# Late modulation vectors as row products on VectorE in a hybrid attention / DeltaNet layer

## The chip, the cores and the metric

The kernel runs on one core of a Trainium2 chip. The metric is the device time of one execution in microseconds (us). The engines are TensorE (PE; its weight loads are listed as PEld), VectorE (DVE), ScalarE (ACT), GpSimd (POOL) and SyncE (SP), which issues the DMAs. Each works through its own queue in order; semaphores tie the queues together.

## The reference, cut to what matters

One layer of a diffusion backbone over 512 latent tokens with a prefix of 256 context tokens, 1024 channels wide, in float32. Two modulation vectors of six parts each are made from the condition vectors `c` and `c_ctx`:

```python
mod_lat = jax.nn.silu(c) @ w_mod + b_mod          # (1, 6144)
mod_ctx = jax.nn.silu(c_ctx) @ w_mod + b_mod
sh1, sc1, g1, sh2, sc2, g2 = jnp.split(mod_lat, 6, axis=-1)
hx = modulate(rms_norm(x), sh1, sc1)              # h * (1 + scale) + shift
...
x = x + g1 * merge_branches(attn_x, gdn_x, gate_x, w_pa, w_pd, w_out)
x = x + g2 * conv_ffn(modulate(rms_norm(x), sh2, sc2), w_up, ffn_conv_w, ffn_conv_b, w_down)
```

The shift and scale of the first sub-layer (`sh1`, `sc1`, columns 0 to 2047 of `w_mod`) are needed at once, for latent and context. The other four parts, `g1`, `sh2`, `sc2`, `g2` (columns 2048 to 6143), are needed only for the latent tokens and only behind the output projection, late in the layer: they are the late modulation vectors. They are 4096 dot products of length 1024 over 16 MB of weights.

Between the two stand the input projection, grouped-query attention (8 query heads, 2 key heads), and a bidirectional chunked gated DeltaNet (8 heads), whose results are merged, projected and followed by a gated MLP.

## The kernel before, in words

All of it is one program for the Tile framework: the source names tiles, pools and operations, and a planner orders each engine's queue by a simulated timeline, from the priority of the instructions (program order, unless a block such as `first()` or `sooner()` raises it) and from when data and buffers are free. `keep_in_program_order` pins an instruction behind the one that stands before it on its engine. `pinned[0]` does so for all PE instructions of a stage. A pool's memory is taken again by the next pool that is opened at its place; with `reuse_waits="tile"` a new tile waits only for the old tiles that it overlaps.

Every large matmul is done in three passes, hi x hi, hi x lo and lo x hi, of operands that ACT and DVE split (`split`, L122; weights in `load_w`, L191: one conversion `whi` on ACT, one subtraction `wlo` on DVE).

The stages in the order of the program:

1. Loads and early modulation (pool `m1`, L415 to L583). `xs`, three tiles of context and latent tokens, are loaded first and normalised; `wm`, eight loads of 1 MB, are the early columns of `w_mod`. The order on PE is written out in `ORD` (L37) and pinned; the loads' order is `LORD`.
2. Key, value and query projection (L698 to L757, pool `kvp`). `blk` 0 is keys, 1 values, 2 to 5 pairs of query heads; there are 28 steps (`blk`, `t`), one for each block and tile of 128 tokens. A step is 24 matmuls into `pq`, then rotary work on DVE and ACT (`qt`, `qtmp`), and the transposes `pt` of the step three before (`LAG`, L54), whose result ACT and DVE split into `KH`/`KL` and `QH`/`QL`. `decays` (L591) runs among the steps: betas and decays of the DeltaNet.
3. Attention (`attend`, L825): for each head and tile of 128 queries, scores into the one bank pair `pS`, maximum on DVE, exponential on ACT, then transposes of the probabilities and products with the values (`ab`). Matmuls of the DeltaNet's projections (`fillA`) are filled in between.
4. The DeltaNet with the other projections, then output projection and MLP, which read the late vectors from columns 16 to 47 of `mod` (L1371 to L1381, L1469).

The late vectors are made by `late_mods` (L362), a generator that stage 2 advances by `MK` = 2.6 steps for each of its 28 steps. For each of eight blocks `q` of 512 columns, `part` (L365) loads eight tiles `wmd` of 128x512 (contraction index on partitions), multiplies each with its column of silu(c) (`csl`) and adds them up: four by DVE, four by ACT with the additions on POOL. Two sums `macc` are added on POOL; `total` (L380) sums over the partitions by a matmul with ones, and ACT copies the row of 512; `columns` (L385) turns it by four transposes of one row each, and DVE adds the bias into `mod`. All of `part` is pinned in program order on its engines (`held`, L359).

Of the kernel before, what the change touches and what calls it, by code (L numbers as in the profile page):

```python
# [6 lines left out]
F32 = mybir.dt.float32  # L7
F32R = mybir.dt.float32r
AF = mybir.ActivationFunctionType
# [38 lines left out]
NS = 2  # L48
MV, MT, CT = 0, 6, 9
MACT, MK, MU = 1, 2.6, 0  # L50
MPIN, MB = 1, 5
DA = '11142332'
# [22 lines left out]
S_BMOD, S_CW, S_FW, S_FB, S_GNW, S_FNW, S_C, S_END = 0, 48, 120, 252, 296, 297, 305, 321  # L75
R_QW, R_QS, R_KW, R_KS, R_A, R_DT, R_END = 0, 128, 256, 384, 512, 528, 544


def hybrid_layer_body(tc, x, ctxt, xT, consts, cols, rows, w_mod1, w_mod2, w_db, w_aq, w_cm, w_pa, w_pd, w_out,
# [39 lines left out]
    def act(out, a, f=AF.Copy, **kw):  # L119
        A.activation(out, a, f, **kw)  # L120
# [10 lines left out]
    def mm(ps, a, b, start=True, stop=True):  # L131
        T.matmul(ps, a, b, start=start, stop=stop)

    with es:
# [34 lines left out]
        modc = cp.tile([P, 16], F32, name="modc")  # L169
        csl = cp.tile([P, KT], F32, name="csl")  # L170

# [14 lines left out]
        def xbank():  # L186
            return xps.tile([P, 4, P], F32, name="xb", tag="x")
# [170 lines left out]

        def held(i):  # L359
            return tc.keep_in_program_order(i) if MPIN else i  # L360

        def late_mods():  # L362
            accs = {}

            def part(q, k):  # L365
                if k == 0:
                    accs[q] = [mdp.tile([P, 512], F32, name="macc", tag="macc", bufs=4) for _ in range(2)]
                av, ap = accs[q]
                wk = mdp.tile([P, 512], F32, name="wmd", tag="wmd", bufs=MB)
                SP.dma_start(wk, w_mod2[q, k // 2][:, (k % 2) * 512:(k % 2) * 512 + 512])  # L370
                if k % 2:
                    held(V.scalar_tensor_tensor(out=av, in0=wk, scalar=csl[:, k:k + 1], in1=av, op0=ALU.mult, op1=ALU.add))
                else:
                    held(A.activation((av, ap, wk)[min(k // 2, 2)], wk, AF.Copy, scale=csl[:, k:k + 1]))
                    if k > 2:
                        held(G.tensor_tensor(out=ap, in0=ap, in1=wk, op=ALU.add))
                if k == KT - 1:
                    held((V if MV else G).tensor_tensor(out=ap, in0=ap, in1=av, op=ALU.add))

            def total(q):  # L380
                ps = xbank()[0:1, :, :].rearrange("p a b -> p (a b)")
                mm(ps, ones[:, 0:1], accs[q][1])
                act(accs[q][0][0:1, :], ps)

            def columns(q):  # L385
                pst = xbank()[:, 0, 0:4]
                for i in range(4):
                    T.transpose(pst[:, i:i + 1], accs[q][0][0:1, i * P:(i + 1) * P], ident[0:1, 0:1])
                tt(mod[:, 16 + 4 * q:20 + 4 * q], pst, col[:, S_BMOD + 16 + 4 * q:S_BMOD + 20 + 4 * q], ALU.add)

            for i in range(9 * KT + CT - 7):
                for at, fn in ((MT, total), (CT, columns)):
                    q = (i - KT - at) // KT
                    if (i - at) % KT == 0 and 0 <= q < 8:
                        fn(q)
                if i < 8 * KT:
                    part(i // KT, i % KT)
                yield

        modact, mods = [MACT], late_mods()  # L400

# [13 lines left out]
        with m1_es:  # L415
# [175 lines left out]
        def decays(g1):  # L591
            rowt = g1.tile([P, 32], F32, name="rowt")
            SP.dma_start(rowt, rows[R_A:R_END].partition_broadcast(P))
            trt = g1.tile([P, 2, P], F32, name="trt")
# [63 lines left out]


        at_es = ExitStack()  # L660
        ap_ = at_es.enter_context(tc.tile_pool(name="ap", bufs=1))
# [7 lines left out]
        with kv_es:  # L669
            mdp = kv_es.enter_context(tc.tile_pool(name="mdp", bufs=1, reuse_waits="tile"))  # L670
            kvp = kv_es.enter_context(tc.tile_pool(name="kvp", bufs=1, reuse_waits="tile"))
# [25 lines left out]

            pend, dec, mcount = [], decays(kvp), 0  # L698
            pinned[0] = KPIN
            for blk in range(6):  # L700
                w2 = [load_w(w_aq[blk, i]) for i in range(2)]
                for t in range(6 if blk < 2 else 4):
# [48 lines left out]
            for i in range(FQ):  # L751
                next(fillA, None)
            for _ in mods:
                pass
            while pend:
# [5 lines left out]
        with at_es:  # L761
# [24 lines left out]
            def probs(h, t, pm):  # L786
                if t == 0:
                    hold["ao"] = at2.tile([P, NL], F32, name="ao", tag="ao", bufs=2)
# [3 lines left out]
                ao, PH, PL = hold["ao"], hold["PH"], hold["PL"]  # L792
                sl = slice((t % 2) * P, (t % 2) * P + P)
# [31 lines left out]
            def attend():  # L825
# [686 lines left out]
def _layout(i):  # L1512
# [32 lines left out]
    a["rows"] = f(np.concatenate([qw, sw(qw), kw, sw(kw), np.asarray(i["a_log"])[0].reshape(-1),  # L1545
                                  np.asarray(i["dt_bias"])[0].reshape(-1)]))
# [37 lines left out]
```

## Time and profile before

| | |
|---|---|
| median of 3 runs | 1305.97 us (1303.61 to 1308.03) |
| the profiled execution | 1306.96 us |
| its span on the core | 1304.3 us |
| mean granted clock of TensorE | 0.978 |
| PE busy | 1229.6 us (94%) |
| DVE busy | 848.4 us (65%) |
| ACT busy | 626.3 us (48%) |
| POOL busy | 308.3 us (24%) |
| DMA | 170.80 MB, 131 GB/s on the mean |

The profile is of one execution. Its span reaches from the first to the last instruction of the program; the time of the execution is a little longer. "Busy" is the time in which an engine worked on at least one instruction; matmuls overlap, so PE is called busy until the modelled end of each. A row of a group gives the line of the source (often that of a helper, such as L87 for a matmul, L108 for `tt`, L117 for `stt`, L120 for `act`), the engine, the operation, the tiles out<-in, the shapes, the count, then busy us and mean ns of one, then idle time of the engine before it and what ended it. The chain of waits is followed back from the last instruction to whatever released each.

### The profile page before, as it was taken

How to read it: one execution, taken by the hardware profiler on the slowest of the kernel's cores; microseconds unless marked ns; L12 is line 12 of the kernel's file. 1: busy time of each engine (PE TensorE's matmuls, PEld its weight loads, DVE VectorE, ACT ScalarE, POOL GpSimd, SP SyncE). 2: the span in 40 equal slices, each digit the busy share in tenths (PEclk: the TensorE clock that was granted, in tenths of full speed). 3: DMA queues.
4: the chain of work that ended last, by engine and by line, in shares of the span. 5: the costliest groups of instructions: out<-in, count | busy, mean ns of one | idle time of the engine just before them, and what ended most of it. 6: DMA issues, size and time to landing. Idle time of an engine off the chain costs nothing.

```text
span 1304.3 us, 20850 instructions
## 1 busy us (share of the span) xinstructions
PE 1229.6 (94%) x7835; PEld 1031.3 (79%) x7835; DVE 848.4 (65%) x1625; ACT 626.3 (48%) x1403; POOL 308.3 (24%) x364
## 2 busy tenths in 40 slices
PE   7899999999968999899998999999999999999997
PEld 4487878999857877778787878788988888888886
DVE  5886987777759986685665556555576666663323
ACT  5453656666576665474453443233354444443221
POOL 1752420000143249559447300000000000000000
PEclk8999999999998999899999999999999999999998
DMA  8656631121373342543533555265043222233331
GB/s 321 227 169 197 223 118 62 65 86 50 111 252 105 124 140 91 177 131 110 178 120 116 170 165 168 92 219 190 9 129 97 97 97 95 91 94 97 90 100 65
DMA packets 70789, 170.80 MB, mean 131 GB/s; under 512 B 7872, under 2 KB 18720, under 8 KB 69280
## 3 DMA queue, kind: packets, MB, share of 16 engines
q1 hardware_dynamic: 70688, 169.47, 39.4%
q8 instruction: 61, 1.00, 0.3%
q14 instruction: 40, 0.33, 0.1%
HBM read 144.23 MB, written 25.21 MB: 130 GB/s over the span
## 4 chain that ended last, share of the span: by engine, by line
PE 66%; POOL 10%; DVE 9%; DMA 5%; ACT 4%; issue 3%; SPq 0%; POOLq 0%; DVEq 0%; ACTq 0%
PE mc L87 32%; PE mb L87 17%; PE pq L87 4%; POOL R L108 4%; POOL prod L108 4%; PE pb L87 3%; PE pS L87 3%; PE ab L87 2%; PE ab L91 1%; DMA Gb<-gamdr 1%; PE xb L91 1%; DVE wlo L108 1%; PE pk L87 1%; DMA sz<-gdr 1%; POOL NN L108 1%
## 5 line engine op out<-in xcount | busy, mean ns | idle before, releaser
L108 DVE TENSOR_TENSOR wlo<-wraw,whi 128x1024 fp32r<-128x1024 f32 x152 | 187.6, 1235 | 162.6 <-ACT whi L120 161.6
L120 ACT ACTIVATE whi<-wraw 128x1024 fp32r<-128x1024 f32 x152 | 159.1, 1048 | 205.5 <-PE mc L87 106.5
L87 PE MATMUL mb<-hxH,whi 128*128 128x512 f32 x384 | 165.1, 430 | 2.1 <-DVE R L108 1.9
L87 PE MATMUL mb<-hxL,whi 128*128 128x512 f32 x384 | 155.0, 404 | 0.0
L87 PE MATMUL mb<-hxH,wlo 128*128 128x512 f32 x384 | 154.3, 402 | 0.0
L87 PE MATMUL mc<-h2L,whi 128*128 128x512 f32 (+1 forms) x376 | 142.7, 379 | 0.0
L87 PE MATMUL mc<-h2H,whi 128*128 128x512 f32 (+1 forms) x376 | 142.3, 378 | 0.3 <-ACT whi L120 0.3
L87 PE MATMUL mc<-h2H,wlo 128*128 128x512 f32 (+1 forms) x376 | 140.8, 374 | 0.5 <-DVE wlo L108 0.5
L108 POOL TENSOR_TENSOR rc<-rc,mhalf 128x2 f32<-128x2 f32 x4 | 3.3, 818 | 459.4 <-DVE rc L114 459.4
L87 PEld LDWEIGHTS mb<-hxH,wlo 128*128 128x128 f32 x384 | 74.0, 193 | 18.3
L87 PEld LDWEIGHTS mb<-hxH,whi 128*128 128x128 f32 x384 | 74.6, 194 | 13.9 <-ACT t L120 2.1
L87 PEld LDWEIGHTS mb<-hxL,whi 128*128 128x128 f32 x384 | 74.6, 194 | 10.3
L87 PEld LDWEIGHTS mc<-h2H,whi 128*128 128x128 f32 x376 | 70.6, 188 | 14.9 <-ACT whi L120 0.5
L87 PEld LDWEIGHTS mc<-h2H,wlo 128*128 128x128 f32 x376 | 70.6, 188 | 14.7 <-DVE wlo L108 1.0
L87 PEld LDWEIGHTS mc<-h2L,whi 128*128 128x128 f32 x376 | 70.7, 188 | 12.2
L87 PE MATMUL mc<-aH,whi 128*128 128x512 f32 (+1 forms) x198 | 72.9, 368 | 0.6 <-DVE x L117 0.6
L87 PE MATMUL mc<-aL,whi 128*128 128x512 f32 (+1 forms) x198 | 73.0, 369 | 0.0
L87 PE MATMUL mc<-aH,wlo 128*128 128x512 f32 (+1 forms) x198 | 72.0, 364 | 0.0
L117 DVE SCALAR_TENSOR_TENSOR u<-mc,col,u 128x511 f32<-128x511 f32 x88 | 65.3, 746 | 1.4
L108 POOL TENSOR_TENSOR prod<-X,R 128x31 f32<-128x31 f32 (+15 forms) x93 | 53.5, 576 | 22.3 <-DVE X L108 15.4
L108 POOL TENSOR_TENSOR R<-R,prod 128x31 f32<-128x31 f32 (+15 forms) x93 | 57.1, 613 | 6.8
L87 PE MATMUL pq<-whi,hxH 128*128 128x256 f32 x192 | 56.6, 295 | 0.0
(354 smaller groups left out, 3078.3 us busy)
## 6 DMA issues: line engine op xcount, KB each, us to landing
wraw<-in_w_cm_dram SPq DMA_DIRECT2D x48, 512.0 KB, 3.9
wraw<-in_w_up_dram SPq DMA_DIRECT2D x44, 512.0 KB, 3.7
wmd<-in_w_mod_dram SPq DMA_DIRECT2D x64, 256.0 KB, 3.8
wm<-in_w_mod_dram SPq DMA_DIRECT2D x8, 1024.0 KB, 8.2
wraw<-in_w_down_dram SPq DMA_DIRECT2D x16, 512.0 KB, 3.5
wraw<-in_w_aq_dram SPq DMA_DIRECT2D x12, 512.0 KB, 4.8
M<-gamdr SPq DMA_DIRECT2D x64, 64.0 KB, 4.4
wraw<-in_w_pa_dram SPq DMA_DIRECT2D x8, 512.0 KB, 4.0
```

Source lines behind the costliest of these rows:

```text
L87: i = nc.tensor.matmul(*a, **k)
L91: i = nc.tensor.transpose(*a, **k)
L108: (eng or V).tensor_tensor(out=out, in0=a, in1=b, op=op)
L117: V.scalar_tensor_tensor(out=out, in0=a, scalar=s, in1=b, op0=op0, op1=op1)
L120: A.activation(out, a, f, **kw)
```

## The change

The late vectors are computed with the channels of the result on the partitions. The host lays out the late columns of `w_mod` transposed: 32 tiles of 128 result channels by 1024. The kernel loads `c` (now a part of `rows`) to all partitions, makes 2 silu(c) there (`cw`), and for each of the 32 tiles DVE does one `scalar_tensor_tensor` that multiplies the tile with `cw` and 0.5 and sums along the row into one column of `ms`. After each eight, one small addition of the bias fills `mod`. The sums on ACT, POOL and PE, the tiles `macc` and `wmd`, and `csl` are gone. The row products are not pinned.

The pool `lm` holds `cw` (4 KB for each partition), `ms` and two buffers for the loads. It is opened behind the early modulation and stays open to the end of attention, below the pools of attention and of the projection. `more_mods` advances the generator by 0.5 for each step of stage 2 and by 0.6 for each tile of attention: one advance for `cw`, then one for each row. To make room, attention's output `ao` is held in tiles of 256 columns and stored in 16 pieces instead of 8.

```diff
+MKV, MAT, MB = .5, .6, 2
-R_QW, R_QS, R_KW, R_KS, R_A, R_DT, R_END = 0, 128, 256, 384, 512, 528, 544
+R_QW, R_QS, R_KW, R_KS, R_A, R_DT, R_C, R_END = 0, 128, 256, 384, 512, 528, 544, 1568
...
-        def late_mods():
...
+        def late_mods(lm):
+            cw = lm.tile([P, D], F32, name="cw")
+            ms = lm.tile([P, 32], F32, name="ms")
+
+            def row():
+                return lm.tile([P, D], F32, name="wl", tag="wl", bufs=MB)
+
+            SP.dma_start(cw, rows[R_C:R_END].partition_broadcast(P))
+            th = row()
+            act(th, cw, AF.Tanh, scale=0.5)
+            stt(cw, th, 1.0, cw, ALU.add, ALU.mult)
+            yield
+            for j in range(32):
+                wl = row()
+                SP.dma_start(wl, w_mod2[j])
+                V.scalar_tensor_tensor(out=wl, in0=wl, scalar=0.5, in1=cw, op0=ALU.mult, op1=ALU.mult, accum_out=ms[:, j:j + 1])
+                if j % 8 == 7:
+                    o = slice(16 + j - 7, 17 + j)
+                    tt(mod[:, o], ms[:, j - 7:j + 1], col[:, S_BMOD + 9 + j:S_BMOD + 17 + j], ALU.add)
                 yield
...
-            V.tensor_copy(csl, cs.rearrange("p (k two) -> p k two", two=2)[:, :, 0])
...
+        lm_es = ExitStack()
+        lm = lm_es.enter_context(tc.tile_pool(name="lm", bufs=1, reuse_waits="tile"))
+        mods, mcount = late_mods(lm), [0.0]
+
+        def more_mods(rate):
+            mcount[0] += rate
+            while mcount[0] >= 1:
+                mcount[0] -= 1
+                next(mods, None)
+
         at_es = ExitStack()
...
-                    if 6 * min(blk, 2) + 4 * max(blk - 2, 0) + t >= MU:
-                        mcount += MK
-                        while mcount >= 1:
-                            mcount -= 1
-                            next(mods, None)
+                    more_mods(MKV)
...
-                    act(ao[:, (t // 2) * 256:(t // 2) * 256 + 256], po)
-                    if t == 3:
-                        SP.dma_start(atd[h], ao)
+                    ao = at2.tile([P, 256], F32, name="ao", tag="ao", bufs=2)
+                    act(ao, po)
+                    SP.dma_start(atd[h][:, (t // 2) * 256:(t // 2) * 256 + 256], ao)
...
                     yield F1
+                    more_mods(MAT)
...
+            for _ in mods:
+                pass
             chunk[0] = CHUNK
             pinned[0] = False
+        lm_es.close()
...
-    a["w_mod2"] = f(wm[:, 2048:].reshape(4, 2, P, 8, 512).transpose(3, 0, 2, 1, 4).reshape(8, 4, P, 1024))
+    a["w_mod2"] = f(wm[:, 2048:].T.reshape(32, P, D))
```

More of the change, by code (lines that the diff above doesn't have):

```diff
@@ L48 @@
 NS = 2
-MV, MT, CT = 0, 6, 9
-MACT, MK, MU = 1, 2.6, 0
-MPIN, MB = 1, 5
+MKV, MAT, MB = .5, .6, 2
 DA = '11142332'
@@ L169, in hybrid_layer_body @@
         modc = cp.tile([P, 16], F32, name="modc")
-        csl = cp.tile([P, KT], F32, name="csl")
         def rsqrt(out, a, s, eps):
@@ L357, in gate_proj @@
                 SP.dma_start(tdr[c], o[:, 0:NL])
-        def held(i):
-            return tc.keep_in_program_order(i) if MPIN else i
-        def late_mods():
[L363 to L397, printed above, removed]
@@ L398, in late_mods @@
                 yield
-        modact, mods = [MACT], late_mods()
         order = [(h + i % 2, part) for h in range(0, NH, 2) for i, part in enumerate((1, 1, 2, 2))]
@@ L592, in decays @@
             rowt = g1.tile([P, 32], F32, name="rowt")
-            SP.dma_start(rowt, rows[R_A:R_END].partition_broadcast(P))
+            SP.dma_start(rowt, rows[R_A:R_C].partition_broadcast(P))
             trt = g1.tile([P, 2, P], F32, name="trt")
@@ L669, in hybrid_layer_body @@
         with kv_es:
-            mdp = kv_es.enter_context(tc.tile_pool(name="mdp", bufs=1, reuse_waits="tile"))
             kvp = kv_es.enter_context(tc.tile_pool(name="kvp", bufs=1, reuse_waits="tile"))
@@ L696, in columns @@
                 split(hi[:, :, ts_], lo[:, :, ts_], pt)
-            pend, dec, mcount = [], decays(kvp), 0
+            pend, dec = [], decays(kvp)
             pinned[0] = KPIN
@@ L752, in hybrid_layer_body @@
                 next(fillA, None)
-            for _ in mods:
-                pass
             while pend:
@@ L786, in probs @@
             def probs(h, t, pm):
-                if t == 0:
-                    hold["ao"] = at2.tile([P, NL], F32, name="ao", tag="ao", bufs=2)
                 if t % 2 == 0:
@@ L791, in probs @@
                     hold["PL"] = at2.tile([P, 6, 256], F32R, name="PL", tag="PL", bufs=2)
-                ao, PH, PL = hold["ao"], hold["PH"], hold["PL"]
+                PH, PL = hold["PH"], hold["PL"]
                 sl = slice((t % 2) * P, (t % 2) * P + P)
@@ L1545, in _layout @@
     a["rows"] = f(np.concatenate([qw, sw(qw), kw, sw(kw), np.asarray(i["a_log"])[0].reshape(-1),
-                                  np.asarray(i["dt_bias"])[0].reshape(-1)]))
+                                  np.asarray(i["dt_bias"])[0].reshape(-1), np.asarray(i["c"])[0]]))
     wm = np.asarray(i["w_mod"])[0]
     a["w_mod1"] = f(wm[:, :2048].reshape(2, 4, P, 2, 4, 256).transpose(4, 0, 2, 1, 3, 5).reshape(4, 2, P, 4, 512))
-    a["w_mod2"] = f(wm[:, 2048:].reshape(4, 2, P, 8, 512).transpose(3, 0, 2, 1, 4).reshape(8, 4, P, 1024))
+    a["w_mod2"] = f(wm[:, 2048:].T.reshape(32, P, D))
     wi = np.asarray(i["w_in"])[0]
```

## The prediction

> **What bounds the kernel now.** I read the page first: span, engines, chain.
>
> ```profile
> span 1304.3 us, 20850 instructions
> PE 1229.6 (94%) x7835; PEld 1031.3 (79%) x7835; DVE 848.4 (65%) x1625; ACT 626.3 (48%) x1403; POOL 308.3 (24%) x364
> PE 66%; POOL 10%; DVE 9%; DMA 5%; ACT 4%; issue 3%; SPq 0%; POOLq 0%; DVEq 0%; ACTq 0%
> ```
>
> Two thirds of the chain of waits is TensorE, so what counts is work taken from PE, or stalls of PE, in the stages that the change touches. A table of windows cuts these into the loads and the early modulation (to 66 us), key and value projection with the decays (to 121.4), query projection (to 186) and attention (to 355). Its columns are the stretch, its length, and busy time with instructions of PE, PEld, DVE, ACT and POOL, then the granted clock, DMA share and GB/s.
>
> ```profile
> 20.00:66.00 46.00, 39.61 (x170) 19.77 (x168) 37.48 (x57) 22.18 (x32) 25.83 (x15) 0.96 0.69 243
> 66.00:121.40 55.40, 51.85 (x385) 45.24 (x385) 40.47 (x91) 26.10 (x66) 22.46 (x19) 1.00 0.54 179
> 121.40:186.00 64.60, 61.99 (x464) 54.43 (x464) 61.43 (x174) 37.63 (x117) 25.96 (x18) 0.97 0.60 195
> 186.00:355.00 169.00, 165.58 (x1114) 148.42 (x1113) 126.06 (x261) 108.24 (x271) 7.67 (x8) 1.00 0.19 69
> ```
>
> Through both projections PE is hardly ever idle (3.6 and 2.6 us). In the query projection DVE is nearly full too (61.4 of 64.6). In attention DVE has 42.9 us free. Next, the chain of waits inside the query projection (start, length, what):
>
> ```profile
> 150.18 2.84 PE pq L87 x24
> 153.02 0.22 PE pt L91 x2
> 153.24 0.33 PE xb L91 x4
> 153.57 3.03 PE pq L87 x24
> ...
> 159.67 0.22 PE pt L91 x2
> 159.89 0.95 PE xb L87 x2
> 160.84 3.03 PE pq L87 x24
> ```
>
> A token tile is 24 matmuls (2.84 to 3.03 us) and two transposes (0.22). Between them sits modulation work on the same PE: a total (0.95 us) and four one-column transposes (0.33 us) for each of the eight column blocks. These are on the chain itself.
>
> **The change part by part.** Removed work, by groups of the stretch 66 to 186 us and by the waits of PE in it:
>
> ```profile
> L87 PE MATMUL xb<-macc,cst 128*1 128x512 f32 x16 | 8.2, 591 | 2.2 <-DVE beta L114 1.7 <-POOL macc L378 0.4
> L91 PE MATMUL xb<-cst,macc 1*128 1x1 f32 x32 | 3.2, 201 | 1.1 <-ACT macc L120 1.1
> L372 DVE SCALAR_TENSOR_TENSOR macc<-wmd,csl,macc 128x512 f32<-128x512 f32 x32 | 28.9, 909 | 2.3 <-DMA wmd<-in_w_mod_dram 2.0 <-ACT macc L374 0.3
> L374 ACT ACTIVATE macc<-wmd,csl 128x512 f32<-128x512 f32 x16 | 11.5, 722 | 7.5 <-DMA wmd<-in_w_mod_dram 7.5
> L376 POOL TENSOR_TENSOR macc<-macc,wmd 128x512 f32<-128x512 f32 x16 | 22.5, 1409 | 35.8 <-ACT wmd L374 30.6 <-DVE s L627 5.0
> ...
> PE xb L91 <- ACT macc L120: 1.8, 2, 1.1
> PE xb L87 <- DVE beta L114: 1.7, 1, 1.7
> ...
> PE xb L87 <- POOL macc L378: 0.4, 1, 0.4
> ```
>
> (1) PE loses eight totals and eight sets of transposes. By the chain that is 8 x (0.95 + 0.33) = 10.2 us; by the groups 8.2 + 3.2 = 11.4, with overlaps. I take 10.2, since the chain's pieces follow one another. (2) PE also loses its waits for those pieces: 1.8 + 1.7 + 0.4 = 3.9 us. They go because the waiting instruction goes. Nothing of the totals stays to be late; the next thing that PE can wait for is the rotary work and the QL split on DVE, which gets freer. Sum: 14.1 us. ACT loses 32 scalings (the L374 row is half of them) and POOL 24 additions; both were idle half of the time, so I cost their removal at nothing. The 64 loads of 256 KB become 32 of 512 KB, half as many issues on SP; the copy csl and the eight evictions of totals on ACT go too, and none of these stands on the chain quoted.
>
> (3) Added: 32 rows on DVE, each one product of 128x1024 with a sum. No such form with a sum on DVE is in the trace. Near rows (ns as min/median/max, then first and last start):
>
> ```profile
> L117 DVE SCALAR_TENSOR_TENSOR co<-co,t x24: 684/954/2315, 73.6 to 588.8; 128x768 f32<-128x768 f32 x16, 128x512 f32<-128x512 f32 x8
> L372 DVE SCALAR_TENSOR_TENSOR macc<-wmd,csl,macc x32: 732/741/1701, 74.5 to 175.6; 128x512 f32<-128x512 f32 x32
> L120 ACT ACTIVATION_READ_ACCUMULATOR qtmp<-pq x44: 189/195/203, 74.8 to 182.8; 128x1 f32 x44
> ```
>
> The same operation takes 684 ns at 512 columns and, by the median of a set that is two thirds 768 columns, 954 ns there: 270 ns for 256 columns, so about 1.22 us at 1024. On ACT the read of a sum costs 0.2 us more. Bounds: 1.2 us (sum free) and 1.8 us (stretched as the L372 mean of 909 against its fastest 732 is, and 0.2 for the sum); I take 1.3, near the undisturbed rows, because POOL, whose additions coincide with the stretched cases, has little left to do. 32 rows are 42 us of DVE, against 28.9 removed. The Vector Engine (DVE) Microarchitecture Reference of the Trainium skill, in "Points that are easy to get wrong", says that this operation with two SBUF sources that are not bf16 runs at half throughput, with no port left for reading the accumulator. The L372 rows are such operations, and their 732 ns for 512 columns does not show a halving against 684; but none of them carries a sum. By the rule the time would be that of the last rival, by the rows that of the forecast.
>
> (4) Added once: a load of c to all partitions (512 KB), a Tanh on ACT and one 128x1024 product on DVE, about 1.1 and 1.2 us by the neighbouring rows. The eight small additions become four. The output of attention leaves in 16 stores instead of 8: eight more issues on SP, read back much later, at nothing; should SP fall behind, it would be the next weight tile that is late.
>
> (5) Where do the rows run? They are written into the loops at 0.5 and 0.6 per step, but unlike the old parts nothing pins them. What an unpinned instruction does is in the trace:
>
> ```profile
> L120 ACT ACTIVATE rowt<-rowt x1: 200/200/200, 74.6 to 74.6; 128x16 f32<-128x16 f32 x1
> L108 DVE TENSOR_TENSOR da<-xb,rowt x2: 197/198/198, 117.6 to 121.1; 128x48 f32<-128x48 f32 x2
> ...
> L91 PE MATMUL pt<-cst,xs x48: 272/421/476, 10.9 to 28.8; 128*128 128x128 f32 x48
> ```
>
> The exponential of rowt is written after the additions of da, yet ran 43 us before the first of them: an instruction goes as soon as its data and memory are there. The new tiles lie where xs0 and xs1 lay (the pool opens at the place of the closed one), and these are free when their transposes are done, within the stretch 10.9 to 28.8. So I expect c's load at about 16 to 20 us and the first row before 30 us, then one pair of rows per load and use of two buffers.
>
> ```profile
> wm<-in_w_mod_dram SPq DMA_DIRECT2D x8, 1024.0 KB, 8.2
> wmd<-in_w_mod_dram SPq DMA_DIRECT2D x64, 256.0 KB, 3.8
> ```
>
> With loads landing after 8.2 us as the large ones of the head do, a pair takes about 8.2 + 1.3 = 9.5 us: from 20 to 66 us some 10 rows. The other 22 follow, at about 3.8 + 2 x 1.3 = 6.4 us a pair, within 70 us: they are through before the query projection ends, and attention sees none. Spare DVE in the projections, with the old products out: (55.4 - 40.5) + (64.6 - 61.4) + 28.9, less the 14 us by which the stretch shrinks, = 33 us, for 22 x 1.3 = 29. They fit under PE, whose products run up to three tiles ahead of its transposes (LAG); without that cover they would cost 29 us.
>
> (6) The head is where rows cost. Between 20 and 66 us DVE has 46 - 37.5 = 8.5 us free; 10 rows and c's product take 14.2: 5.7 us too many. The chain there runs over DVE:
>
> ```profile
> 47.79 2.00 ACT wmh L120 x2
> 49.81 2.64 DVE wml L108
> ...
> 52.79 2.65 DVE hf L114 x2
> 55.68 3.13 POOL hf L114 x2
> ```
>
> A row in front of wml or hf on DVE's queue delays these, and behind them the gemv of PE; its wait for a load holds the same queue. On SP a row's load waits for the row two before it, and behind it stand the loads of wm; c's Tanh on ACT holds the conversions of whi and hxH. Bounds: 0 (no row floats so far) and 14.2 (each stands on the chain). I take 5, near the excess.
>
> Sum against the profiled execution, 1306.96 us (span 1304.3 and 2.7 around it): 1306.96 - 10.2 - 3.9 + 5 = 1297.9. The median of the three runs, 1305.97, lies 1.0 below that execution, so I predict **1296.9**. The likeliest case's own range: rows free in the head gives 1292, the head at 11 instead of 5 gives 1303.
>
> **The rivals.** *The rows stay spread as written.* Then 19 run in attention: 24.7 us of DVE into 42.9 free. For it: the rates are in the code. Against: the rowt row. In attention these waits show how tight the loop is:
>
> ```profile
> DVE mx L821 <- ACT pm L120: 16.4, 25, 1.4
> DVE mx L817 <- PE pS L87: 10.5, 18, 1.1
> ```
>
> In 18 of 32 tiles DVE starts its maximum the moment the scores land, and PE cannot overwrite the one score bank before the exponential; a row in the way delays both, by up to 1.3 us. At 0.4 us a row, 19 x 0.4 = 8 us; none is paid in the head: 1306.96 - 14.1 + 8 - 1 = 1299.9. If every row cost its 1.3 us, 1316.6.
>
> *The head pays for all of it (slower).* Place: DVE's in-order queue between 20 and 75 us. Price: each row that reaches DVE before its load has landed holds wml, hf and wlo behind it. The chain shows one such wait, for a buffer and its load:
>
> ```profile
> 74.58 0.68 DVE macc L372
> ...
> 75.27 5.02 DMA wmd<-in_w_mod_dram
> ```
>
> Ten rows at 1.3 us, two waits of 3 to 5 us, with loads that share the queue of wm: about 20 us. 1306.96 - 14.1 + 20 - 1 = 1311.9. It decides from a head cost above 14.1 us, 1.4 us a row. For it: wm loads take 8.2 us there, and POOL is busy 25.8 of 46 us in the same stretch, so products stretch. Against: there is some free time.
>
> *The head pays nothing.* Rows find gaps, or the loads keep to their places: 1306.96 - 14.1 - 1 = 1291.9. For it: POOL and ACT are relieved, so the rotary work speeds up. Against: 8.5 us free for 14.2.
>
> *A sum costs a second pass.* If summing took a second pass over the sources, a row would be 1.22 + 4 x 0.27 = 2.3 us. At that, 32 rows take 74 us; beyond the 33 + 8.5 free some 32 us remain, which spill into attention: 14 rows there, at 0.8 us, 11 us, and 9 us in the head: 1306.96 - 14.1 + 20 - 1 = 1311.9, the same number by another way. Against it: the co rows show one pass. (The Trainium skill's rule of part (3) is this case.)
>
> **How the numbers follow.** Chances: forecast 0.46, head free 0.16, spread 0.16, head pays all 0.17, second pass 0.05. What can be told from no change is about 0.3%, 3.9 us: 1302.1 to 1309.9. Faster: 0.42 of the forecast, all 0.16 of the free head, 0.09 of the spread: 0.67. Same: 0.04, 0.05 and 0.04 of the slow head: 0.13. Slower: 0.02 of the spread and 0.18 of the slow cases: 0.20. The range for 8 in 10 goes from 1288 (head free and more of PE's idle time gone) to 1310; the likeliest case's own is 1292 to 1303.
>
> **What would show it.** The query and key matmuls begin here (the first start is what matters):
>
> ```profile
> L87 PE MATMUL pq<-whi,hcH x32: 277/280/384, 70.3 to 97.2; 128*128 128x256 f32 x32
> ```
>
> Right: the first new product on DVE before 35 us, the last before 190; the query projection's tiles at 2.8 to 3.1 us with nothing between them but two transposes; attention at 169 us as before; the first pq a few us later than 70.3. A first row after 66 us proves step (5) wrong; a row mean over 1.8 us proves step (3) wrong; first pq after 84 us is the slow rival; attention over 173 us is the spread one.

## The result and the profile after

The changed kernel takes **1325.64 us** (median of 4 runs, 1324.44 to 1326.17) against 1304.79 us (1302.84 to 1308.03) for the kernel before on the same chip: a ratio of 1.0158, 95% interval 1.0142 to 1.0174. It is slower by 1.6%; the prediction said 1296.9, range 1288 to 1310.

The page of the changed kernel, first lines and shares of the chain of waits:

```profile
span 1324.0 us, 20648 instructions
PE 1226.5 (93%) x7787; PEld 1032.0 (78%) x7787; DVE 844.5 (64%) x1653; ACT 601.7 (45%) x1364; POOL 273.8 (21%) x340
PE 62%; POOL 10%; DVE 9%; DMA 7%; ACT 5%; issue 3%; SPq 1%; POOLq 0%; DVEq 0%; ACTq 0%
```

TensorE has lost 48 instructions, and VectorE is busy no longer than it was (844.5 us, 848.4 before); DMA has gained two points of the chain. The shares don't say where the time went; the table of windows does, with the same columns as in the prediction and cut where the stages now change:

```profile
20.00:66.00 46.00, 39.28 (x171) 20.17 (x169) 37.49 (x57) 21.02 (x31) 26.44 (x14) 0.96 0.67 241
66.00:121.40 55.40, 50.79 (x385) 46.50 (x383) 41.63 (x102) 15.55 (x48) 7.41 (x9) 0.97 0.59 185
121.40:201.50 80.10, 55.15 (x414) 53.91 (x414) 61.37 (x188) 24.81 (x96) 7.46 (x4) 0.84 0.50 161
201.50:372.00 170.50, 166.78 (x1112) 149.13 (x1111) 126.61 (x259) 108.01 (x271) 10.61 (x9) 0.99 0.19 68
```

The head (to 66 us) is unchanged. The stretch from 121.4 us to the first scores has grown from 64.6 to 80.1 us, with TensorE idle for 25 of them, and its mean granted clock there (the share of full clock that the profile records) fell from 0.97 to 0.84. The rows themselves, by groups of the changed kernel (ns as min/median/max, then first and last start):

```profile
L372 DVE SCALAR_TENSOR_TENSOR wl<-wl,cw x32: 1212/1224/1227, 76.1 to 168.6; 128x1024 f32<-128x1024 f32 x32
L372 DVE DVE_READ_ACCUMULATOR wl<-wl,cw x32: 78/82/84, 77.2 to 169.7; 128x1 f32 x32
L364 SPq DMA_DIRECT2D cw<-in_rows_dram x1: 427/427/427, 58.0 to 58.0; - x1
```

A row is 1.22 us and 0.08 for its sum. All 32 rows run between 76 and 170 us: none in the head, none in attention. First starts and last ends of such groups give the stages of the table below, in which every kernel of the study is set out. "Projections" is from the first `pq` to the first `pS`, "attention" from there to the last `ab`, "middle" from there to the first `mc`, and "mc" (output projection and MLP) from its first to its last product.

| kernel (profiled execution) | span | first pq | projections | attention | middle | mc |
|---|---|---|---|---|---|---|
| before | 1304.3 | 70.4 | 115.6 | 168.9 | 524.2 | 418.8 |
| changed | 1324.0 | 69.6 | 131.9 | 170.7 | 518.9 | 426.4 |
| changed, 32 bytes | 1318.6 | 70.4 | 130.9 | 169.9 | 522.2 | 418.8 |
| before, 96 bytes | 1311.1 | 69.9 | 113.8 | 169.7 | 524.8 | 426.1 |
| before, 64 bytes | 1302.9 | 70.3 | 113.8 | 168.9 | 527.2 | 416.0 |
| rows pinned | 1317.7 | 70.2 | 106.5 | 190.3 | 517.6 | 426.5 |
| one load | 1313.3 | 70.2 | 120.4 | 171.4 | 518.3 | 426.5 |
| decays later | 1312.6 | 70.3 | 118.5 | 170.3 | 520.8 | 426.0 |
| both of these | 1306.7 | 70.8 | 112.3 | 170.4 | 520.2 | 426.5 |
| half on GpSimd | 1312.0 | 70.3 | 125.7 | 170.7 | 519.9 | 419.0 |
| most on GpSimd | 1315.2 | 70.4 | 129.2 | 169.9 | 521.0 | 418.5 |
| before, columns | 1308.3 | 70.0 | 119.8 | 169.8 | 523.8 | 418.5 |
| no rows | 1284.7 | 70.8 | 97.8 | 171.5 | 519.8 | 418.5 |
| late, GpSimd | 1316.8 | 69.4 | 98.4 | 169.9 | 549.0 | 423.7 |
| late, VectorE | 1295.0 | 68.7 | 98.4 | 169.9 | 532.2 | 419.2 |
| late, VectorE, 96 bytes | 1297.6 | 69.6 | 97.9 | 170.5 | 536.7 | 416.0 |

So the changed kernel loses 16.3 us in the projections, 1.8 in attention and 7.6 in mc, and gains 0.8 ahead and 5.3 in the middle: 19.6 of the 19.7 us by which the spans differ. The gain in the middle was not traced to a cause. What TensorE waits for in the projections, by waits (us in total, times, longest):

```profile
PE mb L85 <- DVE da L110: 15.9, 1, 15.9
PE pq L85 <- DVE wlo L106: 7.8, 3, 5.0
PE pt L89 <- DVE QL L106: 3.1, 1, 3.1
PE pq L85 <- DVE rk L112: 2.6, 1, 2.6
...
DVE wl L372 <- DMA wl<-in_w_mod_dram: 22.5, 18, 2.1
```

Before, no single wait of TensorE in this stage was over 1.7 us. VectorE's order during the longest one (start, length, what; the bracket is idle time ahead of the instruction and what ended it):

```profile
143.85 0.25 DVE L115 SCALAR_TENSOR_TENSOR pl<-pl,s 128x96 f32<-128x96 f32 x1
...
146.78 1.23 DVE L372 SCALAR_TENSOR_TENSOR wl<-wl,cw 128x1024 f32<-128x1024 f32 x1 [1.80 <-DMA wl<-in_w_mod_dram]
147.93 0.08 DVE L372 DVE_READ_ACCUMULATOR wl<-wl,cw 128x1 f32 x1
147.93 0.25 DVE L115 SCALAR_TENSOR_TENSOR pl<-pl,s 128x96 f32<-128x96 f32 x1
148.10 0.16 DVE L106 TENSOR_TENSOR mod<-ms,col 128x8 f32<-128x8 f32 x1
148.17 1.22 DVE L372 SCALAR_TENSOR_TENSOR wl<-wl,cw 128x1024 f32<-128x1024 f32 x1
149.32 0.08 DVE L372 DVE_READ_ACCUMULATOR wl<-wl,cw 128x1 f32 x1
149.32 0.26 DVE L115 SCALAR_TENSOR_TENSOR pl<-pl,s 128x96 f32<-128x96 f32 x1
```

`pl` and `da` are the chain of small operations in `decays`, some 0.2 to 0.3 us each. Between its links stand rows of 1.3 us, and a row also waits for its load. Meanwhile TensorE stands still at the first product that needs `da` (the window, same columns):

```profile
137.00:153.00 16.00, 0.11 (x2) 0.11 (x1) 12.85 (x38) 1.55 (x6) 2.48 (x1) 0.66 0.72 229
```

The chain of waits through this part of the projections shows the other half, the load of each pair of rows following the products of the pair before, since there are two buffers:

```profile
101.06 4.53 DMA wl<-in_w_mod_dram
105.68 1.24 DVE wl L372 x2
106.94 3.99 DMA wl<-in_w_mod_dram
111.03 1.23 DVE wl L372 x2
...
149.43 4.83 DMA wl<-in_w_mod_dram
154.28 1.23 DVE wl L372 x2
155.54 4.83 DMA wl<-in_w_mod_dram
```

### The profile page after: what moved, and what is told of

It is laid out like the page before. It is cut to its first block, busy times and chain, and to the rows that moved or that the text cites. A ratio compares the mean times of both kernels' runs of the same rounds, so it can differ in the third digit from the quotient of the medians.

```text
span 1324.0 us, 20648 instructions
## 1 busy us (share of the span) xinstructions
PE 1226.5 (93%) x7787; PEld 1032.0 (78%) x7787; DVE 844.5 (64%) x1653; ACT 601.7 (45%) x1364; POOL 273.8 (21%) x340
## 4 chain that ended last, share of the span: by engine, by line
PE 62%; POOL 10%; DVE 9%; DMA 7%; ACT 5%; issue 3%; SPq 1%; POOLq 0%; DVEq 0%; ACTq 0%
PE mc L85 32%; PE mb L85 16%; POOL prod L106 4%; POOL R L106 4%; PE pb L85 3%; DMA wl<-in_w_mod_dram 3%; PE pS L85 3%; PE pq L85 3%; PE ab L85 2%; PE ab L89 1%; DVE wl L372 1%; DVE wlo L106 1%; DMA Gb<-gamdr 1%; DMA sz<-gdr 1%; POOL Gb L106 1%
## 5 line engine op out<-in xcount | busy, mean ns | idle before, releaser
L106 DVE TENSOR_TENSOR wlo<-wraw,whi 128x1024 fp32r<-128x1024 f32 x152 | 187.6, 1236 | 170.4 <-ACT whi L118 169.1
L85 PE MATMUL mc<-h2H,wlo 128*128 128x512 f32 (+1 forms) x376 | 144.5, 384 | 0.5 <-DVE wlo L106 0.5
L85 PEld LDWEIGHTS mb<-hxH,whi 128*128 128x128 f32 x384 | 74.8, 195 | 14.1 <-issue 3.7
L85 PE MATMUL pq<-wlo,hxH 128*128 128x256 f32 x192 | 56.6, 295 | 7.3 <-DVE wlo L106 7.3
L106 POOL TENSOR_TENSOR prod<-X,R 128x31 f32<-128x31 f32 (+15 forms) x93 | 56.6, 608 | 19.9 <-DVE X L106 13.0
```

The lines of the kernel that those rows point to most:

```text
L85: i = nc.tensor.matmul(*a, **k)
L106: (eng or V).tensor_tensor(out=out, in0=a, in1=b, op=op)
```

## The experiments

The theories at the outset: (A) the 7.6 us in mc come from the place of the weight tiles, which moved when `csl` went; (B) the rows hold VectorE's queue while their loads are on the way; (C) the products themselves are more than VectorE can take in.

**The place of the weight tiles.** By the layout of the program the pool of the weight tiles (`wraw`, `whi`, `wlo`) began at byte 24512 of a partition before and begins at 24480 after, because `csl`, 32 bytes, is gone. Modulo 128 that is 64 and 32. (The two bytes are counted from the program's tiles; no run prints them. What the edits fix is the distance from the old place: 32 bytes less in the change, then 0, 96 and 64 bytes more.) The first edit puts the 32 bytes back into the changed kernel; the second puts the old kernel's tiles at 32 modulo 128, the third at 0.

```diff
+pad = cp.tile([P, 8], F32, name="pad")    # changed kernel; 24 and 16 columns in the kernel before
+V.memset(pad, 0.0)
```

> The changed kernel with one unused tile of 32 bytes per partition, which puts the weight tiles of the output projection and the MLP back on the addresses that they had before the change (without the tile csl they had moved down by 32 bytes). Theory A (the move of 32 bytes makes the products with those tiles slower): the stretch from the first to the last product of the block mc goes back from 426.4 to about 418.8 us, the query projection stays as long as it is (131.9 us from first pq to first pS), and the time is about 1318. Rival (the 7.6 us there have another cause): the stretch stays at 426, the time at about 1325.

> The kernel before with one unused tile of 96 bytes per partition, which puts those weight tiles where the change puts them, counted modulo 128 bytes; nothing else differs. Theory A: the stretch of mc goes up from 418.8 to about 426 us, the time from 1305 to about 1312. Rival: both stay.

> The kernel before with one unused tile of 64 bytes, so that the weight tiles lie 64 bytes further and keep their place modulo 64, not modulo 128. If it is the place modulo 64 that counts (32 is slow, 0 is not), the mc stretch stays at 418.8 us and the time at 1305; if every move from the old place costs, or the place modulo 128, the stretch is 426 or otherwise off 418.8 and the time with it.

Measured: 1320.33 us for the first (ratio to before 1.0129, 1.0099 to 1.0159), 1312.23 for the second (1.0047, 1.0029 to 1.0065), 1303.52 for the third (0.9981, 0.9966 to 0.9996). One group of the MLP in the changed kernel, then in the first, second and third of these:

```profile
L85 PE MATMUL mc<-h2H,wlo x376: 276/399/497, 937.6 to 1186.7; 128*128 128x512 f32 x164, 128*128 128x256 f32 x24
```

```profile
L85 PE MATMUL mc<-h2H,wlo x376: 275/388/497, 939.5 to 1183.8; 128*128 128x512 f32 x164, 128*128 128x256 f32 x24
```

```profile
L87 PE MATMUL mc<-h2H,wlo x376: 276/396/497, 924.8 to 1173.7; 128*128 128x512 f32 x164, 128*128 128x256 f32 x24
```

```profile
L87 PE MATMUL mc<-h2H,wlo x376: 279/389/499, 926.0 to 1168.6; 128*128 128x512 f32 x164, 128*128 128x256 f32 x24
```

First to last start of the same products: 249.1 us at place 32, 244.3 back at 64, 248.9 in the old kernel at 32, 242.6 at 0. (The median of one group does not rank the places: it is 388 at place 64 and 389 at 0. The first to last start does.) Theory A holds both ways round. The third contradicts the place modulo 64, and of the other alternative only the loose part holds, "otherwise off 418.8": the stretch is 416.0, shorter than before. That the period is 128 bytes rests on one pair, the distances of 32 less and 96 more, with 426.4 and 426.1 us. The projections stayed long in the first run (130.9), so the place explains mc and nothing else.

**Rows in the order of the code.**

```diff
-V.scalar_tensor_tensor(out=wl, ..., accum_out=ms[:, j:j + 1])
+tc.keep_in_program_order(V.scalar_tensor_tensor(out=wl, ..., accum_out=ms[:, j:j + 1]))
```

> The changed kernel with the 32 row products kept in the order of the code on VectorE, so 13 are done in the projections and 19 in attention. Theory B (in the changed kernel the rows hold VectorE's queue while their loads are under way, and the rotary work, the decays and so TensorE wait behind them): first pq to first pS falls from 131.9 to about 104 us, since only 13 rows come there, 4 us or more apart; attention goes from 170.7 to 172 to 178 us; the mc stretch stays at 426; time 1298 to 1312. Rival C (the products themselves, 42 us of VectorE, are what is too much): the projections still shrink, by the 19 rows that leave them, but attention pays for them in full, 19 x 1.3 = 25 us: 195 us, time about 1322.

Measured: 1320.27 us (1.0122, 1.0100 to 1.0144). The projections fall to 106.5 us as theory B has it, but attention takes 190.3, where theory C put 195. Waits of the attention stage in this kernel:

```profile
PEld pS L85 <- ACT pm L118: 14.3, 11, 2.4
ACT pm L118 <- DVE mx L115: 14.0, 10, 4.8
...
DVE wl L372 <- DMA wl<-in_w_mod_dram: 3.7, 3, 2.0
```

Hardly any wait for loads is left, and yet the loop is late: the row delays the maximum, that the exponential, and that the scores of the next tile (before, `PEld pS` waited 1.0 us for it). Against the 171.5 us of a kernel without rows, shown below, 19 rows cost 18.8 us, 0.99 us each. Theory B as it stood is not enough. In the projections the other 13 rows cost 106.5 us less the 97.8 of the same kernel without rows, 8.7 us or 0.67 each: the price of a row is no fixed figure.

**Products without loads.**

```diff
+wl = row()
+SP.dma_start(wl, w_mod2[0])
 for j in range(32):
-    wl = row()
-    SP.dma_start(wl, w_mod2[j])
-    V.scalar_tensor_tensor(out=wl, in0=wl, ...)
+    V.scalar_tensor_tensor(out=th, in0=wl, ...)
```

> The changed kernel with one load of a weight tile in place of 32: all 32 products read this one tile (31 loads are left out, so the late modulation vectors are not those of the reference). The products stay, 1.3 us each, and none has to wait for a load. Theory B: first pq to first pS falls from 131.9 to 100 to 105 us, though the same 42 us of products run on VectorE. Rival C: it stays above 120 us. If the rows then run early, before 66 us, the first pq is later than 69.6 us by what the head pays.

Measured: 1315.11 us (one execution); projections 120.4, on rival C's side by a hair. Loads cost 11.5 us of the 131.9. The longest wait of TensorE stayed:

```profile
PE mb L85 <- DVE da L110: 16.6, 1, 16.6
```

**Shared products.** All rows in the projections, pinned, with three buffers and the 32 bytes; some of the products on GpSimd, with their sum by a copy on ScalarE (`j % 4` in the second).

```diff
+if j % 2:
+    held(G.tensor_tensor(out=wl, in0=wl, in1=cw, op=ALU.mult))
+    sums.append((j, wl))           # summed two rows later, A.activation(..., AF.Copy, accum_out=...)
+else:
+    held(V.scalar_tensor_tensor(...))
```

> All 32 rows in the projections and in the order of the code (1.4 a tile, three buffers, the unused 32 bytes of the first experiment in place), but only 16 of the products on VectorE with their sum; the other 16 are multiplied on GpSimd and summed by a copy on ScalarE. Theory D (TensorE's gain is real, and it was the sum of VectorE's work and its order that ate it): TensorE still needs about 101 us in the projections, VectorE 70 + 21 = 91 us, GpSimd 12 + 16 x 2.8 = 57, ScalarE 39 + 20 = 59; first pq to first pS 102 to 106 us (115.6 before, 131.9 changed), attention 169, time 1293 to 1297. Rival E (what costs is rows as such, by their loads into few buffers and waits of engines for them, whatever engine multiplies): 112 us or more, time above 1304.

> As the half split, but with 24 of the 32 products on GpSimd and 8 on VectorE. Theory D: VectorE 70 + 10 = 80 us, GpSimd 12 + 67 = 79, ScalarE 39 + 30 = 69 of about 102: first pq to first pS 101 to 106 us, time 1292 to 1297. Rival E: GpSimd's 2.8 us a product hold the three buffers longer, rows and the loads get later, 110 us or more, time above 1302.

Measured: 1315.21 us (1.0083, 1.0065 to 1.0100) and 1316.84 us (1.0084, 1.0063 to 1.0105), projections 125.7 and 129.2 us. Theory D's numbers fail, and the sizes put for rival E (112 us or more, above 1304) come out. TensorE in the first of them:

```profile
PE mb L85 <- DVE da L110: 11.2, 1, 11.2
PE pq L85 <- DVE wlo L106: 8.7, 3, 4.6
PE pt L89 <- DVE QL L106: 4.4, 2, 3.1
```

It still waits for VectorE, though VectorE has only half of the rows. And VectorE is as busy as with all of them: 102.4 us of the projections here and 104.6 in the second, with 8 rows, against 101.2 in the changed kernel; theory D had put 91 and 80. Why showed itself later, in the kernel with late rows on GpSimd.

**Decays later in TensorE's order.**

```diff
-DA = '11142332'
+DA = '11144352'
```

> The changed kernel with the third and fourth part of the decays (their products on TensorE, and what follows) moved from the first and second block of the query projection to its third and fourth, so TensorE meets the product that waits for da some 25 us later in its order; the rows stay as they are. Theory F (rows set between the links of the decays' chain on VectorE make da late by 16 us, and TensorE waits for it): first pq to first pS falls by 12 to 16 us, from 131.9 to 116 to 120, the same loads and products all the same; time about 1312. Rival C (VectorE's total is the bound, so the wait only moves): above 125 us, time about 1322.

Measured: 1314.35 us (one execution); projections 118.5, wait for `da` 3.6 us:

```profile
PE pq L85 <- DVE wlo L106: 6.6, 3, 5.1
PE mb L85 <- DVE da L110: 3.6, 1, 3.6
```

Theory F holds, by one execution: 13.4 us of the 131.9 go with one wait for one chain that the rows stretched.

**Another sum on TensorE, in the kernel before.**

```diff
 def total(q):
-    ...
+    pass
 def columns(q):
     pst = xbank()[:, 0, 0:4]
     for i in range(4):
-        T.transpose(pst[:, i:i + 1], accs[q][0][0:1, i * P:(i + 1) * P], ident[0:1, 0:1])
+        mm(pst[:, i:i + 1], accs[q][1][:, i * P:(i + 1) * P], ones[:, 0:1])
```

> The kernel before (its sums on three engines) with the eight totals and the 32 transposes replaced: each block's summed tile is the stationary side of four products with one column of ones, so the four columns of a block come out at once, without the row of totals and its copy on ScalarE. If TensorE's time in those pieces (0.95 + 0.33 us a block) is what the modulation costs on the path, four products of one column at some 0.1 to 0.25 us each save 0.3 to 0.9 us a block, with the 1.1 us waited for the copy: 3 to 8 us, time 1298 to 1303. Rival: the weight load of a 128x128 f32 tile is no shorter than what went, and nothing is saved: 1305.

Measured: 1311.24 us (1.0049, 1.0034 to 1.0065), so slower, which neither alternative had: projections 119.8. The sums became 64 short products (a f32 product here is two instructions), and TensorE met `da` before it was ready:

```profile
L87 PE MATMUL xb<-cst,macc x64: 167/250/250, 93.7 to 185.9; 128*128 128x1 f32 x64
```

```profile
PE mb L87 <- DVE da L112: 8.7, 1, 8.7
```

**No rows at all**, with the 32 bytes: the ceiling of the gain.

```diff
-for j in range(32):
-    ...
+V.memset(mod[:, 16:48], 0.5)
```

> The changed kernel with the unused 32 bytes and without the 32 loads, products and sums: the late modulation vectors are set to a constant (this part of the computation is left out), while c is still loaded and put through Tanh and its product. So TensorE has lost the totals and transposes and nothing is added. Theory D: first pq to first pS is 115.6 - 14.1 = 101.5 us, attention 169, mc 418.8, time 1291 to 1293; the gain of the prediction's first two steps is there. Rival G (TensorE's pieces were cover for VectorE's chain of the decays, which then shows as a wait of TensorE in their place): 105 us or more, with a wait of mb for da over 4 us, time 1296 or more.

Measured: 1283.25 us (0.9830, 0.9808 to 0.9852), projections 97.8. The gain is larger than forecast (1291 to 1293), and the wait for `da` is gone, so rival G falls. TensorE needs 98 us there, and VectorE 68 (31.45 + 36.34):

```profile
66.00:121.40 55.40, 54.82 (x431) 51.00 (x432) 31.45 (x90) 18.51 (x60) 8.54 (x10) 1.00 0.16 53
121.40:168.60 47.20, 43.77 (x372) 43.30 (x371) 36.34 (x135) 21.94 (x84) 6.12 (x4) 1.00 0.28 84
```

With this as the base the 32 rows of the changed kernel cost 131.9 - 97.8 = 34.1 us in the projections, loads included, 1.07 us each. By the two traces 26 us of that is TensorE standing idle (29.6 us against 3.4) and 8 us is TensorE taking longer over the same products (busy 102.3 against 94.4 us, mean granted clock 0.89 against 1.00).

**Rows at the end of the DeltaNet stage, on GpSimd.** The pool opens behind `hx_es.close()` on the right side; a row is taken every fourth step of the projections pa and pd.

```diff
+def spread(g):
+    for i, w in enumerate(g):
+        if i % MEV == 0:
+            next(mods, None)
+        yield w
-yield from paired(w_pa, 0, atn, finish_pa)
+yield from spread(paired(w_pa, 0, atn, finish_pa))
```

> The rows as in the change, but from the end of the DeltaNet stage (the projections pa and pd, some 765 to 880 us, where GpSimd is hardly busy), four steps of head products apart, each multiplied on GpSimd and summed by a copy on ScalarE, with three buffers and the unused 32 bytes; the query projection and attention have none. Theory D: the front is as in the kernel without rows (first pq to first pS about 101.5 us, attention 169), and the late stage pays little, since the rows stand on engines that nothing there waits for: 32 x 2.8 = 90 us of GpSimd in 120 us, 32 x 1.25 = 40 us of ScalarE; time 1292 to 1298, faster than both. Rival E (rows cost wherever they stand, through the queue of SyncE, the loads and ScalarE's order): the stretch from 760 us to the first mc grows by 10 us or more and takes the gain back: 1303 or more.

Measured: 1317.63 us (1.0087, 1.0066 to 1.0107). The front is as without rows, but the middle takes 549.0 us, 29 more than without rows: rival E's size. The cause is in the timeline. VectorE, then GpSimd, in this kernel:

```profile
839.79 2.76 DVE L106 TENSOR_TENSOR g_m<-sz,g_k 128x512 fp32r<-128x512 f32 x1 [0.69 <-ACT g_k L118]
843.86 0.69 DVE L115 SCALAR_TENSOR_TENSOR gd<-gd,mb 128x512 f32<-128x512 f32 x1 [1.31 <-PE mb L85]
844.59 2.93 DVE L106 TENSOR_TENSOR gd<-gd,ga 128x512 f32<-128x512 f32 x1
847.44 3.43 DVE L106 TENSOR_TENSOR wlo<-wraw,whi 128x1024 fp32r<-128x1024 f32 x1
```

```profile
839.64 2.36 POOL L380 TENSOR_TENSOR wl<-wl,cw 128x1024 f32<-128x1024 f32 x1 [6.60 <-DMA wl<-in_w_mod_dram]
844.57 5.22 POOL L380 TENSOR_TENSOR wl<-wl,cw 128x1024 f32<-128x1024 f32 x2 [2.57 <-ACT whi L118]
```

The two operations on `gd` over the whole kernel (ns as min/median/max):

```profile
L115 DVE SCALAR_TENSOR_TENSOR gd<-gd,mb x8: 671/680/689, 843.9 to 889.3; 128x512 f32<-128x512 f32 x8
L106 DVE TENSOR_TENSOR gd<-gd,ga x8: 679/1538/2933, 844.6 to 890.0; 128x512 f32<-128x512 f32 x8
```

The addition `gd<-gd,ga`, with both operands in SBUF, takes 0.68 us when GpSimd is idle, and 2.93 when a product of GpSimd has just begun: 2.4 us for that product to end and then about its own time. `g_m` and `wlo` are stretched in the same way, to 2.76 and 3.43 us. `gd<-gd,mb` reads one operand from PSUM: four of its eight met a product of GpSimd and still took 0.67 to 0.69 us. So a product on GpSimd does not add an engine: it takes VectorE's time for operations on two SBUF operands. From 735 us to the first `mc` VectorE is busy 111.1 us here, with none of the rows, and 72.3 in the kernel without rows. The rival that the sums on ScalarE hold TensorE up finds little in the trace: from 700 us to the first `mc` TensorE waits 19.7 us for VectorE (5.4 without rows) and 3.9 for ScalarE (2.5). In the half split, too, a row on VectorE took up to 3.14 us beside a median of 1.21. The Trainium skill has this rule (SBUF — State Buffer, section "SBUF: two separate sides"): VectorE and GpSimd share a pair of ports; between a VectorE operation with two SBUF inputs and a GpSimd operation that reads SBUF, whoever begins first holds it for the whole instruction, and the other is blocked. These rows agree.

**Late rows on VectorE**, one to five steps, the rest in the output projection:

```diff
-held(G.tensor_tensor(out=wl[j - 1], in0=wl[j - 1], in1=cw, op=ALU.mult))
+held(V.scalar_tensor_tensor(out=w, in0=w, scalar=0.5, in1=cw, ..., accum_out=ms[:, j - 1:j]))
```

> As the last kernel, but each row is one product with its sum on VectorE, as in the change; GpSimd and ScalarE have none of it. One row to five steps of head products, so some 25 rows come between 740 and 880 us and the rest in the output projection. In that stretch VectorE is busy 69 of 120 us without rows, and gets 25 x 1.3 = 33 us more. Theory H (a product on GpSimd stops VectorE for its 2.4 us, which is what the last kernel paid for; a row on VectorE costs only where VectorE sets the pace): first pq to first pS 98 us, the first mc at about 865 to 870 us (859.9 without rows), 0.2 to 0.4 us a row, time 1290 to 1298, faster than both. Rival I (a row costs about 1.1 us wherever it stands, as in the projections and in attention): first mc at 885 or later, time 1315 or more.

Measured: 1299.94 us (0.9951, 0.9933 to 0.9970), faster than both kernels, by 0.5% than the one before. The same rows:

```profile
L375 DVE SCALAR_TENSOR_TENSOR wl<-wl,cw x32: 1211/1219/1226, 740.1 to 904.0; 128x1024 f32<-128x1024 f32 x32
```

Theory H: first `mc` at 869.2 us, as put. By the spans the 32 rows cost 1295.0 - 1284.7 = 10.3 us, 0.3 each; by the medians 16.7, 0.5 each. The median is past the 1290 to 1298 that was put and 0.5 is above the 0.2 to 0.4, so the low price is not as well measured as its difference from 1.07.

**Two parts of the 34 us at once.** One load for all products, and the decays later:

> The changed kernel with both earlier edits: one weight tile loaded for all 32 products (31 loads are left out, so the late modulation vectors are not those of the reference), and the decays' third and fourth part in the third and fourth block of the query projection. If the two costs are separate they add: 131.9 - 11.5 - 13.4 = 107 us from first pq to first pS, time about 1304. If the two edits remove the same delay: 116 to 120 us, time about 1313, and what is left over 97.8 is VectorE's work itself.

Measured: 1307.54 us (1.0000, 0.9985 to 1.0016), projections 112.3, between the two cases. The loads and the decays alone save 11.5 and 13.4 us, together 19.6: about 5 us were the same delay. The other 14.5 us over the kernel without rows remain though no row waits for a load any more; TensorE still waits 7.2 us for `da`. With the loads out, what is left to cause them is the products on VectorE, and the instructions that stand behind them; how they divide further was not tried.

**The best of it**: late rows on VectorE, with 24 columns of padding, so that the weight tiles lie at a multiple of 128.

> The kernel with the rows late on VectorE, with an unused tile of 96 bytes in place of 32, which puts the weight tiles at a multiple of 128 bytes. If the place works here as it did in the kernel before (418.8 to 416.0 us for mc), 3 us less than 1299.9: about 1297, 0.6 to 0.7% under the kernel before. If not, 1300.

Measured: **1295.77 us** (0.9904, 0.9884 to 0.9923), mc 416.0 us: both findings add up, 4.2 us by the medians where 3 was put. (The two profiled executions alone don't show it, since the middle stage of this one is 4.5 us longer; the medians do.)

## Why the prediction was wrong

**Steps (1) and (2), TensorE's gain**: right in kind, too small. The sum had 14.1 us; without rows the projections are 17.8 us shorter and the whole 19.6 by the spans. Counted in the two traces from each product's start to the next one's, less the idle time between, the totals and transposes in `xb` fell from 11.0 to 0.5 us, which bears out the chain's 10.2. TensorE's idle time fell by 2.6 us (6.0 to 3.4) where 3.9 was put, since the waits behind `QL` and `qt`, 0.8 us before, came to 3.4. The other 4.7 us or so, which the sum did not have, are the products that stayed (`pq` 83.8 to 81.0 us, `pt` 5.9 to 3.9); why they run quicker was not tried.

**Step (3), the price of a row**: right. 1.224 + 0.082 = 1.31 us against 1.3. The second pass did not occur: 1024 columns with a sum take 1224 ns, where two f32 SBUF sources without a sum took 684 ns for 512. So the rule of the Trainium skill named there, read as a price on the sum, is not seen here. That page of the Trainium skill does not say against what the throughput is halved, and its halving against bf16 sources no run here could show: none has such a row. For the same reason the prediction's own test, 732 against 684, decides nothing, since the `co` rows too have two f32 sources.

**Step (4)**: nothing in the runs speaks against it; the 16 stores were not tried alone.

**Step (5), where the rows run and what they cost: this step failed**, in two ways. First, its place in time: c's load was to go out at 16 to 20 us. It went out at 58.0, since SyncE's queue held it behind the weight loads of the projections (start, length, what, then waits of SyncE between 40 and 76 us):

```profile
43.73 14.22 SPq L194 DMA_DIRECT2D wraw<-in_w_aq_dram  x3
58.00 0.43 SPq L364 DMA_DIRECT2D cw<-in_rows_dram  x1
```

```profile
SPq L194 <- DVE wlo L106: 13.9, 3, 9.0
```

The trace lists no wait of c's load itself: it was the queue that was not free. The load took 5.2 us to land, and its Tanh then ran only at 72.1 us, some 9 us later, in ScalarE's order behind work that waited for TensorE. The first row at 76.1 us is past the 66 us that the prediction gave as the mark against this step. Second, and this is the 34 us: "they fit under PE". That was a sum of idle time, 33 us free for 29, and it left VectorE 96% full (40.5 + 61.4 - 28.9 + 29 of 106 us). Since no row ran in the head, it was not 22 rows but all 32 that came, 42 us for the 33. The excess alone is not the cost: in the changed kernel VectorE is busy 101.2 of 131.9 us, so it was idle for some 30 us and late all the same. Idle time in a queue that works in order is free only where nothing behind a row is waited for. Here the decays' chain, the split `wlo` and the rotary work stood behind rows, and behind these TensorE. The sentence on the head, that a row which comes before its load holds the instructions behind it, named part of the mechanism, but set it before 66 us only. VectorE waited so 18 times in the projections, 22.5 us in all. The prediction's own words, "without that cover they would cost 29 us", are near the 34 us that were paid, but by luck: the 29 stood for 22 rows at 1.3 us, and 32 were paid at 1.07.

**Step (6), the head**: 5 us were taken, none was paid (first `pq` 69.6 against 70.4), since no row got there.

**The rivals.** The rows did not stay spread; when they were pinned, attention cost 1.0 us a row, not the 0.4 that was put, and the bound "if every row cost its 1.3 us" was nearer. The slow rival had part of the mechanism, rows that wait for their loads, at the wrong place: without those loads 120.4 of the 131.9 us remained.

**What no step had**: 7.6 us from the place of the weight tiles, since the prediction put the copy into `csl` at nothing and did not ask what lay behind its 32 bytes. Without it the changed kernel is still slower (1320.33). Against the span forecast to shrink by 9.1 us (14.1 less 5) and grown by 19.7, the parts are: 34.1 for the rows where 0 was put, 17.8 gained where 14.1 was put, the head 0.8 shorter where 5 more were put, 7.6 in mc, 1.8 in attention, and the unexplained 5.3 gained in the middle.

## What to carry to other kernels

Idle time of an engine is no room for new work in its queue: look for what stands behind the new instruction and who waits for that, and put the work in a stage in which that answer is nobody, or hardly anybody. A product moved to GpSimd may be VectorE's time all the same. After any change of a pool, compare the spacing of matmuls in a stage that was not touched.

## What the hardware showed beyond that

The same products took 242.6, 244.3 to 244.5 and 248.9 to 249.1 us at places 0, 64 and 32 of their weight tiles modulo 128 bytes, in two kernels; `h2H`, `h2L`, `aH` and `aL` are laid at multiples of 2048, so their place modulo 128 is the same in all. That it is the reading of the weights, and not of another tile that moved with them, is only argued. A VectorE operation on two SBUF operands that met a product of GpSimd (2.4 us) waited for its end: 0.68 us became 2.93. One that read an operand from PSUM did not: 0.67 to 0.69 us beside such products.
